# Two queues for the first transfers, and x ahead of the last memory blocks, in a two-layer hybrid attention kernel

## The chip, the cores and the metric

The kernel runs on one core of one Trainium2 chip. The metric is device time in microseconds of one execution; the runs of the kernel before took 297.54, 295.9 and 296.98 us, so the median is 296.98. Five engines work side by side, each in its own order: TensorE (PE; PEld are its weight loads), VectorE (DVE), ScalarE (ACT), GpSimd (POOL) and SyncE (SP), which here only issues transfers.

## The reference, cut to what matters

```python
def hybrid_layer(x, mem, norm_g, w_in, w_out, mem_norm_g, w_mem_kv, qk_g):
    h = rms_norm(x, norm_g)
    proj = jnp.einsum('btd,de->bte', h, w_in)
    ...
    a_q, a_k, a_v, a_g, b_q, b_k, b_v, b_g, m_q, m_g = jnp.split(proj, cuts, axis=-1)
    ...
    mkv = jnp.einsum('bmd,de->bme', rms_norm(mem, mem_norm_g), w_mem_kv)
    m_k, m_v = jnp.split(mkv, 2, axis=-1)
    qm = rms_norm(to_heads(m_q, N_HEADS_MEM), qk_g[4])
    km = rms_norm(to_heads(m_k, N_HEADS_MEM), qk_g[5])
    om = from_heads(memory_attention(qm, km, to_heads(m_v, N_HEADS_MEM)))

    y = jnp.concatenate([oa * jax.nn.silu(a_g), ob * jax.nn.silu(b_g), om * jax.nn.silu(m_g)], axis=-1)
    return x + jnp.einsum('bte,ed->btd', y, w_out)
```

Two such layers run one after the other. x and mem are 256 tokens of 1,024 columns in float32. Three kinds of attention (causal, dilated, and over the memory) share the projections of x; the memory's keys and values come from a projection of mem of their own.

## The kernel before, in words

Every product of activations and weights is made of three products of parts: an operand is split into a high part (`hi`, `xmh`; ScalarE casts it to a 12-bit form) and a low part (`lo`, `xml`; VectorE subtracts), and TensorE adds high x high, low x high and high x low (`products`, line 142). Weights arrive as raw tiles, one `raw` tile per unit, from a ring of three buffers (`RAW_BUFS`), are split (`split`, line 409; `hi` at line 422, `lo` at line 423), and used. A raw buffer is free again when the `lo` that reads it is done.

The projections stand in a fixed order: mkv (keys and values of the memory, 512 columns, two units of four row blocks), mq and mg (the memory attention's queries and gate, one unit of 1,024 KB each), then bq, bk, and so on (384 columns, two units each). The transfers stand in that order on SP, which issues them in order: one that waits for a free buffer holds those behind it.

The head of the first layer is the place of the change. The transposed memory (`memT`) comes in eight blocks of 128 rows, x in two halves of 128 tokens. All of it goes through SP: memory blocks and kv weights in turn, then x, then mq and mg, the untransposed memory, gains, bq. TensorE first runs 17 transposes of the identity (`warm`). The first four row blocks of mkv are then multiplied in float32 as they come (`whole`, line 477), the last four by parts: memory blocks 4 and 5, then 6 and 7 are split (`split_x`, line 174), and the weights with them. Then x's rows are scaled (`row_scale` and `normed_rows`: a square with a sum on ScalarE, `ms` on VectorE, a power on GpSimd, and `xn` on VectorE), transposed by TensorE in four groups of four (`transposed`), and split into `xmh` and `xml`. The scaled copy `xn` takes a buffer of the raw ring.

Behind this the memory attention starts: mq's two accumulators are squared, normalised and scaled (`normed`, line 253: `sq`, `hss`, `ms`, `hrs`, `t`, `qn`), then the keys (`kn`), and both are transposed (`pair_of_heads`, line 277) between the products of bq. Accumulators come from four PSUM banks (`acc`), so bq's take those of mq. Instructions passed through `pin` and `keep_in_program_order` stay in the order in which the code writes them; the other places are set by a scheduler when the program is built. TensorE's order is wholly that of the code.

Of the kernel before, what the change touches and what calls it, by code (L numbers as in the profile page):

```python
# [10 lines left out]
F32 = mybir.dt.float32  # L11
# [19 lines left out]
# microseconds of TensorE's own clock until a step of attention may follow  # L31
# [6 lines left out]
# Constants of the shapes alone: masks (an additive log of how many patterns hold a key) and rope tables.  # L38
# [26 lines left out]
def hybrid_kernel(ctx: ExitStack, tc: tile.TileContext, x, mem, mem_t, gains, w_in, w_out, w_mem_kv, qk_g, const, out):  # L65
# [11 lines left out]
    # ---- constants made on chip  # L77
# [4 lines left out]
    nc.scalar.activation(cp.tile([P, 16], F32, name="table"), mhalf, AF.Square)  # L82
    pinning = [True]

    def pin(ins):
        """Holds an instruction in its place in the order of its engine, where that is asked for."""
        return tc.keep_in_program_order(ins) if pinning[0] else ins
# [11 lines left out]
    def pe(ins, us):  # L99
        """TensorE follows the trace; its clock tells when what waits for other engines may come next."""  # L100
        tc.keep_in_program_order(ins)
        clock[0] += us
# [11 lines left out]
    def keep_warm(n):  # L114
        """TensorE's clock rises while it is busy."""
        for _ in range(n):
            pe(nc.tensor.transpose(warm[:, 0:P], ident, ident), 0)
# [3 lines left out]
    def poll():  # L121
        """The steps of attention whose operands should be there by now."""
# [19 lines left out]
    def products(groups, first, last, x_moves=False):  # L142
        """acc += x w by block of rows, x and w in two parts each: all products but that of the low parts."""
# [10 lines left out]
    def row_scale(src, t, name, junk):  # L154
        """rsqrt of the mean square of each token's row."""
# [9 lines left out]
    def transposed(src, k2, spare=False):  # L165
        """Two column blocks of both token tiles, by [column, token]."""
# [7 lines left out]
    def split_x(dst, v, g, k2):  # L174
        """Two column blocks, by [column, token], times the gains, in two parts of 12 bits each."""
# [9 lines left out]
    # ---- constants  # L185
# [7 lines left out]
    def prepare_tables(l):  # L193
        """A layer's gains times cosines and sines, the scale of the scores with those of the queries."""
# [17 lines left out]
    def project(xs, chunk, n):  # L212
        """Both token tiles times a chunk of columns."""
# [17 lines left out]
    def project_t(xs, chunk, n):  # L231
        """A chunk of columns of both token tiles, by [column, token]."""
# [20 lines left out]
    def normed(acc, n, dst, tables):  # L253
        """dst = the rms-normed (and rotated) heads of acc."""
# [22 lines left out]
    def pair_of_heads(qn, kn, pair, masks, v, gate, ready, finished):  # L277
        """Queries and keys by [dim, token]; then both heads, whose values share the columns of TensorE."""
# [43 lines left out]
    def head(me, s, spans, masks, pTs):  # L322
        """Softmax of a head, by [key, query] in the end."""
# [33 lines left out]
    # ---- the projections, in the order in which their weights come  # L357
# [12 lines left out]
    units = []  # (chunk, first row block, row blocks, columns)  # L370
# [8 lines left out]
    splits = []  # (unit, first row block, row blocks, columns)  # L379
# [5 lines left out]
    def loads():  # L385
        while loaded[0] < len(units):
# [12 lines left out]
            for b in range(0, nk, step):  # L399
                e = b + step  # L400
                pin(nc.sync.dma_start(raws[u][:, b:e],
                                      src[(a + b) * P:(a + e) * P, :].rearrange("(k p) n -> p k n", p=P)))
# [8 lines left out]
    def split(upto):  # L411
        """Weights in two parts of 12 bits each."""
# [15 lines left out]
    def weights():  # L428
        """The parts of the next chunk, one after another; those behind are under way."""
# [8 lines left out]
    # ---- the first arrivals, in the order of their use  # L438
    for k in range(KD):
        if k < 2 or k % 2 == 0:  # L440
            load_mem(k, k + 1 if k < 2 else k + 2)
        if k == 0:
            pin(nc.sync.dma_start(gT, gains))
        if k < 4 or k % 2 == 0:
            next(loading)
    for t in range(NT):
        pin(nc.sync.dma_start(x_sb[:, t], x[t * P:(t + 1) * P]))
    load(RAW_BUFS + 1)
# [7 lines left out]
    def next_mem(dst, g):  # L456
        """The next layer's memory, bit by bit."""
# [6 lines left out]
    for l in range(DEPTH):  # L464
        gx = gT[:, 8 * l:8 * l + 8]
        xn = wp.tile([P, NT, D], F32, tag="raw", name="xn", bufs=RAW_BUFS)
# [175 lines left out]
```

## Time and profile before

| | us |
|---|---|
| median of three runs | 296.98 |
| profiled execution, first to last instruction (span) | 296.5 |
| TensorE busy | 288.6 (97% of the span) |
| VectorE busy | 203.5 (69%) |
| ScalarE busy | 198.3 (67%) |
| GpSimd busy | 55.7 (19%) |

The profiled execution gives its span alone, 296.5 us; the timed runs lie between 295.9 and 297.54. A wait of an engine is named by who ended it. Matmul ends are modelled and a matmul overlaps the next one's start, so the starts of weight loads are the better clock for TensorE. The granted clock is shown as 1.00 in all stretches quoted.

### The profile page before, as it was taken

The numbers are of one execution on the slowest core, as the hardware profiler recorded it, in microseconds if no ns is written. First come the engines' busy times: TensorE is split into PE (matmuls) and PEld (weight loads), VectorE is DVE, ScalarE is ACT, GpSimd is POOL, SyncE is SP. The second block draws the span as 40 slices with busy tenths as digits, with TensorE's granted clock in tenths as the row PEclk, the third lists the DMA queues.
The fourth block names the chain that finished last, engine by engine and source line by source line (L and its number), as shares of the span: only waits on it lengthen the run. The fifth ranks groups of instructions, "written<-read, shape, count | busy, mean of one in ns | idle before, by whom it ended". The sixth has DMA issues, their size and how long they took to land.

```text
span 296.5 us, 4973 instructions
## 1 busy us (share of the span) xinstructions
PE 288.6 (97%) x1809; PEld 250.6 (85%) x1809; DVE 203.5 (69%) x454; ACT 198.3 (67%) x442; POOL 55.7 (19%) x73
## 2 busy tenths in 40 slices
PE   8989989999999999999999999999999999999994
PEld 6469989698988999977788999989898899987773
DVE  1468899977656997654475759879665699666413
ACT  2578888796878656988364654878587864698600
POOL 0013489130000330000001048703000023000000
PEclk9999999999999999999999999999999999999999
DMA  5999568235438067254307635650823715821003
GB/s 166 375 372 346 186 199 249 70 109 166 155 106 249 19 196 273 97 198 167 118 0 249 211 110 135 223 153 26 262 64 110 239 41 173 300 75 53 3 0 142
DMA packets 32777, 47.33 MB, mean 160 GB/s; under 512 B 1264, under 2 KB 27632, under 8 KB 32752
## 3 DMA queue, kind: packets, MB, share of 16 engines
q1 hardware_dynamic: 32752, 47.01, 48.6%
q8 instruction: 14, 0.23, 0.3%
q14 instruction: 11, 0.09, 0.1%
HBM read 45.96 MB, written 1.05 MB: 159 GB/s over the span
## 4 chain that ended last, share of the span: by engine, by line
PE 81%; DMA 7%; DVE 6%; ACT 2%; POOL 1%; issue 1%; SPq 1%; DVEq 0%; ACTq 0%
PE acc L107 65%; PE wk L110 8%; PE o L107 5%; PE wk L107 5%; DMA x_sb<-in_x_dram 3%; DMA raw<-in_w_in_dram 3%; DVE lo L423 2%; DMA raw<-in_w_mem_kv_dram 2%; POOL hrs L152 1%; DVE hss L259 1%; ACT hi L422 1%; DVE xn L454 0%; DVE ms L151 0%; ACT xn L157 0%; POOL r L152 0%
## 5 line engine op out<-in xcount | busy, mean ns | idle before, releaser
L423 DVE TENSOR_TENSOR lo<-raw,hi 128x768 fp32r<-128x768 f32 (+1 forms) x90 | 96.1, 1089 | 33.6 <-ACT hi L422 33.6
L422 ACT CAST hi<-raw 128x768 fp32r<-128x768 f32 (+1 forms) x90 | 82.9, 936 | 38.2 <-PE acc L107 25.8
L107 PE MATMUL acc<-hi,xmh 128*128 128x384 f32 (+2 forms) x248 | 66.1, 348 | 0.0
L107 PE MATMUL acc<-hi,xml 128*128 128x384 f32 (+2 forms) x248 | 62.7, 335 | 0.8 <-DVE xml L182 0.8
L107 PE MATMUL acc<-lo,xmh 128*128 128x384 f32 (+2 forms) x248 | 62.6, 334 | 0.0
L152 POOL TENSOR_TENSOR hrs<-ms,mhalf 128x6 f32<-128x6 f32 (+1 forms) x24 | 30.3, 1262 | 119.6 <-DVE ms L151 119.1
L107 PEld LDWEIGHTS acc<-hi,xmh 128*128 128x128 f32 x248 | 41.9, 189 | 5.3 <-issue 3.0
L107 PEld LDWEIGHTS acc<-hi,xml 128*128 128x128 f32 x248 | 44.1, 188 | 2.2 <-DVE xml L182 1.2
L107 PEld LDWEIGHTS acc<-lo,xmh 128*128 128x128 f32 x248 | 44.2, 188 | 1.0
L107 PE MATMUL acc<-hi,yT 128*128 128x512 f32 x128 | 41.5, 406 | 0.0
L107 PE MATMUL acc<-xmh,hi 128*128 128x256 f32 x128 | 29.7, 293 | 0.0
L337 ACT ACTIVATE pr<-pr,nm 128x128 f32<-128x128 f32 (+1 forms) x48 | 21.4, 446 | 12.2 <-DVE nm L335 12.2
L107 PE MATMUL acc<-xml,hi 128*128 128x256 f32 x128 | 28.4, 283 | 0.0
L107 PE MATMUL acc<-xmh,lo 128*128 128x256 f32 x128 | 28.4, 283 | 0.0
L107 PEld LDWEIGHTS acc<-hi,yT 128*128 128x128 f32 x128 | 23.0, 188 | 5.2 <-issue 0.7
L343 ACT ACTIVATE pr<-pr,rinv 128x128 f32<-128x128 f32 (+1 forms) x64 | 25.6, 461 | 0.0
L107 PE MATMUL acc<-lo,yT 128*128 128x512 f32 x64 | 25.3, 395 | 0.0
L107 PEld LDWEIGHTS acc<-xmh,hi 128*128 128x128 f32 x128 | 20.9, 191 | 0.7 <-issue 0.7
L107 PEld LDWEIGHTS acc<-xml,hi 128*128 128x128 f32 x128 | 21.1, 191 | 0.0
L107 PEld LDWEIGHTS acc<-xmh,lo 128*128 128x128 f32 x128 | 21.1, 191 | 0.0
L354 ACT COPY pT<-wk 128x384 f32<-128x384 f32 (+1 forms) x32 | 15.4, 503 | 6.5 <-PE wk L110 6.5
L335 DVE CUSTOM_DVE_ANT_0 pr<-wk,cst 128x128 f32<-128x128 f32 (+1 forms) x48 | 14.3, 353 | 5.3 <-PE wk L107 5.3
(75 smaller groups left out, 361.9 us busy)
## 6 DMA issues: line engine op xcount, KB each, us to landing
raw<-in_w_in_dram SPq DMA_DIRECT2D x24, 768.0 KB, 4.9
raw<-in_w_in_dram SPq DMA_DIRECT2D x8, 1024.0 KB, 5.5
raw<-in_w_out_dram SPq DMA_DIRECT2D x6, 1024.0 KB, 6.1
raw<-in_w_in_dram SPq DMA_DIRECT2D x4, 512.0 KB, 3.6
raw<-in_w_out_dram SPq DMA_DIRECT2D x4, 512.0 KB, 4.4
raw<-in_w_mem_kv_dram SPq DMA_DIRECT2D x2, 1024.0 KB, 5.0
raw<-in_w_mem_kv_dram SPq DMA_DIRECT2D x4, 256.0 KB, 4.9
raw<-in_w_mem_kv_dram SPq DMA_DIRECT2D x2, 512.0 KB, 7.2
```

The source lines that it names most:

```text
L107: pe(nc.tensor.matmul(out, a, b, start=start, stop=stop), us)
L110: pe(nc.tensor.transpose(out, a, ident), 0.109)
L152: pin(nc.gpsimd.tensor_tensor(dst, ms, mhalf[:, :n], op=ALU.pow))
L259: pin(nc.vector.tensor_reduce(ss, heads(sq), axis=AX.X, op=ALU.add))
L335: nc.vector.tensor_tensor_reduce(out=pr[:, spans[t]], in0=s[:, spans[t]], in1=masks[t], scale=-1.0, scalar=3e38, op0=ALU.add, op1=ALU.min, ...
L337: nc.scalar.activation(pr[:, spans[t]], pr[:, spans[t]], AF.Exp, scale=-1.0, bias=nm[:, t:t + 1], accum_out=sums[:, t:t + 1])
L343: nc.scalar.activation(pr[:, spans[t]], pr[:, spans[t]], AF.Copy, scale=rinv[:, t:t + 1])
L354: nc.scalar.copy(pT[:, :n], ps[:, :n])
L422: pin(nc.scalar.copy(hi, raw))
L423: pin(nc.vector.tensor_tensor(lo, raw, hi.bitcast(F32), op=ALU.subtract))
```

## The change

The six transfers of mkv's weights of the first layer are issued by ScalarE instead of SP, ahead of everything else there; the small activation that loads ScalarE's table moves behind them. On SP the halves of x stand ahead of memory blocks 4 and 5, and 6 and 7. The scaled copy of x in the first layer lies in a tile of the tag `yT1` rather than in the raw ring. The square, the scale and `xn` of each half of x are written between the splits of the last memory blocks, and TensorE transposes x ahead of the products of memory blocks 6 and 7. Splits of mq's weights follow the first two groups of x's parts. The rest of the diff takes out comments.

```diff
@@ -74,16 +74,15 @@
     mhalf = cp.tile([P, 16], F32, name="mhalf")
     nc.vector.memset(mhalf, -0.5)
-    nc.scalar.activation(cp.tile([P, 16], F32, name="table"), mhalf, AF.Square)
     pinning = [True]
...
@@ -398,8 +397,9 @@
             step = 1 if u == 0 else 2 if u == 1 else nk
             for b in range(0, nk, step):
                 e = b + step
-                pin(nc.sync.dma_start(raws[u][:, b:e],
-                                      src[(a + b) * P:(a + e) * P, :].rearrange("(k p) n -> p k n", p=P)))
+                queue = nc.scalar if u < 2 else nc.sync
+                pin(queue.dma_start(raws[u][:, b:e],
+                                    src[(a + b) * P:(a + e) * P, :].rearrange("(k p) n -> p k n", p=P)))
                 yield
 
     loading = loads()
...
@@ -435,16 +435,18 @@
             split(s + ahead[0])
             yield splits[s][1], splits[s][2], parts[s]
 
-    # ---- the first arrivals, in the order of their use
-    for k in range(KD):
-        if k < 2 or k % 2 == 0:
-            load_mem(k, k + 1 if k < 2 else k + 2)
-        if k == 0:
-            pin(nc.sync.dma_start(gT, gains))
-        if k < 4 or k % 2 == 0:
-            next(loading)
+
+    load(2)
+    next(loading)
+    nc.scalar.activation(cp.tile([P, 16], F32, name="table"), mhalf, AF.Square)
+    load_mem(0, 1)
+    pin(nc.sync.dma_start(gT, gains))
+    load_mem(1, 2)
+    load_mem(2, 4)
     for t in range(NT):
         pin(nc.sync.dma_start(x_sb[:, t], x[t * P:(t + 1) * P]))
+        load_mem(4 + 2 * t, 6 + 2 * t)
+    first_xn = sp.tile([P, NT, D], F32, tag="yT1", name="xn", bufs=1)
     load(RAW_BUFS + 1)
     pin(nc.sync.dma_start(mem_sb, mem.rearrange("(t p) c -> p t c", p=P)))
     load_gains(4, 6)
...
@@ -463,31 +465,33 @@
 
     for l in range(DEPTH):
         gx = gT[:, 8 * l:8 * l + 8]
-        xn = wp.tile([P, NT, D], F32, tag="raw", name="xn", bufs=RAW_BUFS)
+        xn = wp.tile([P, NT, D], F32, tag="raw", name="xn", bufs=RAW_BUFS) if l else first_xn
         xs = xm_tiles()
         if l == 0:
-            # the order of the arrivals, which holds every engine to it
+
             mem_xs = xm_tiles()
             whole.append(cp.tile([P, 4, T], F32, name="whole"))
             mkv, steps = project(mem_xs, weights(), 512)
             r_mem = []
             g = gT[:, 16:24]
             for k in range(4):
-                # float32 as it comes, while the parts of what follows are made
+
                 pin(nc.vector.tensor_scalar(whole[0][:, k], memT[:, k], g[:, k:k + 1], None, op0=ALU.mult))
                 next(steps)
-            for k2 in (4, 6):
+            for t, k2 in enumerate((4, 6)):
+                r = row_scale(x_sb, t, "r", xn[:, t])
                 split_x(mem_xs, memT[:, k2:k2 + 2], g, k2)
-                split(k2 // 2 + 1)
-            for t in range(NT):
-                normed_rows(t, xn)
-            split(SPLIT_BUFS)
-            for _ in range(2):
-                next(steps)
-            for k2 in range(0, KD, 2):
-                if k2 == 2:
-                    split(SPLIT_BUFS + 1)
-                split_x(xs, transposed(xn, k2, k2 == 6), gx, k2)
+                if t == 0:
+                    split(3)
+                pin(nc.vector.tensor_scalar(xn[:, t], x_sb[:, t], r, None, op0=ALU.mult))
+            split(4)
+            next(steps)
+            turned = [transposed(xn, k2, k2 == 6) for k2 in range(0, KD, 2)]
+            next(steps)
+            for k2, v in zip(range(0, KD, 2), turned):
+                split_x(xs, v, gx, k2)
+                if k2 < 4:
+                    split(SPLIT_BUFS + k2 // 2)
             mem_gain = gB[:, :, 4]
             pin(nc.gpsimd.tensor_scalar(mem_gain, mem_gain, 0.125, None, op0=ALU.mult))
             ahead[0] = SPLIT_BUFS - 1
```

What the scheduler makes of it follows at three places. The first is the head of SP's queue, where `memT` are the memory blocks and `raw<-in_w_mem_kv_dram` the kv weights; before:

```order
L95 DMA memT<-in_mem_t_dram 128x256
L443 DMA gT<-in_gains_dram 128x32
L401 DMA raw<-in_w_mem_kv_dram 128x512
L95 DMA memT<-in_mem_t_dram 128x256
L401 DMA raw<-in_w_mem_kv_dram 128x512
L95 DMA memT<-in_mem_t_dram 128x2x256
L401 DMA raw<-in_w_mem_kv_dram 128x512 x2
L95 DMA memT<-in_mem_t_dram 128x2x256
L401 DMA raw<-in_w_mem_kv_dram 128x2x512
L95 DMA memT<-in_mem_t_dram 128x2x256
L401 DMA raw<-in_w_mem_kv_dram 128x2x512
L447 DMA x_sb<-in_x_dram 128x1024 x2
L401 DMA raw<-in_w_in_dram 128x8x256 x2
```

And with the change, SP, and ScalarE's head beside it:

```order
L94 DMA memT<-in_mem_t_dram 128x256
L443 DMA gT<-in_gains_dram 128x32
L94 DMA memT<-in_mem_t_dram 128x256
L94 DMA memT<-in_mem_t_dram 128x2x256
L447 DMA x_sb<-in_x_dram 128x1024
L94 DMA memT<-in_mem_t_dram 128x2x256
L447 DMA x_sb<-in_x_dram 128x1024
L94 DMA memT<-in_mem_t_dram 128x2x256
L401 DMA raw<-in_w_in_dram 128x8x256 x2
```

```order
L401 DMA raw<-in_w_mem_kv_dram 128x512 x4
L401 DMA raw<-in_w_mem_kv_dram 128x2x512 x2
L441 ACT_TABLE_LOAD
L441 ACTIVATE table<-mhalf 128x16
L156 ACTIVATE xn,ss<-x_sb 128x1024
L178 ACTIVATE xmh<-memT,gT 128x256 x2
L422 CAST hi<-raw 128x1024
```

All kv weights went from SP to ScalarE, and x's halves stand third and second from the end of the first group on SP, each ahead of two memory blocks.

The second place is VectorE's head, from the float32 blocks (`whole`) to the first parts of x (`xml<-wk`); `lo<-raw,hi` are low parts of weights, `xn` is x scaled. Before, and with the change:

```order
L477 TENSOR_SCALAR whole<-memT,gT 128x256 x4
L182 SCALAR_TENSOR_TENSOR xml<-memT,gT,xmh 128x256 x2
L423 TENSOR_TENSOR lo<-raw,hi 128x1024
L182 SCALAR_TENSOR_TENSOR xml<-memT,gT,xmh 128x256 x2
L423 TENSOR_TENSOR lo<-raw,hi 128x1024
L151 TENSOR_SCALAR ms<-ss 128x1
L454 TENSOR_SCALAR xn<-x_sb,r 128x1024
L151 TENSOR_SCALAR ms<-ss 128x1
L454 TENSOR_SCALAR xn<-x_sb,r 128x1024
L423 TENSOR_TENSOR lo<-raw,hi 128x1024
L182 SCALAR_TENSOR_TENSOR xml<-wk,gT,xmh 128x256 x2
```

```order
L479 TENSOR_SCALAR whole<-memT,gT 128x256 x4
L150 TENSOR_SCALAR ms<-ss 128x1
L181 SCALAR_TENSOR_TENSOR xml<-memT,gT,xmh 128x256 x2
L423 TENSOR_TENSOR lo<-raw,hi 128x1024
L486 TENSOR_SCALAR xn<-x_sb,r 128x1024
L150 TENSOR_SCALAR ms<-ss 128x1
L181 SCALAR_TENSOR_TENSOR xml<-memT,gT,xmh 128x256 x2
L486 TENSOR_SCALAR xn<-x_sb,r 128x1024
L423 TENSOR_TENSOR lo<-raw,hi 128x1024
L181 SCALAR_TENSOR_TENSOR xml<-wk,gT,xmh 128x256 x2
L423 TENSOR_TENSOR lo<-raw,hi 128x1024
```

The second `lo`, that of mkv's last two row blocks, stood ahead of both `xn` and stands behind both, and the square's follow-up `ms` of each half moved up between the splits of the memory blocks.

The third place is VectorE from the low parts of mg (`128x1024 x2`) to the normalisation of the memory's queries (`hss`, `t`, `qn`); `lo<-raw,hi 128x768` are low parts of bq. Before, and with the change:

```order
L423 TENSOR_TENSOR lo<-raw,hi 128x1024 x2
L151 TENSOR_SCALAR ms<-ss 128x1
L423 TENSOR_TENSOR lo<-raw,hi 128x768
L259 TENSOR_REDUCE hss<-sq 128x4
L151 TENSOR_SCALAR ms<-hss 128x4
L263 TENSOR_TENSOR t_336<-acc,gB 128x256
L273 TENSOR_TENSOR qn<-t_336,hrs 128x256
L259 TENSOR_REDUCE hss<-sq 128x4
L151 TENSOR_SCALAR ms<-hss 128x4
L263 TENSOR_TENSOR t_347<-acc,gB 128x256
L423 TENSOR_TENSOR lo<-raw,hi 128x768
```

```order
L423 TENSOR_TENSOR lo<-raw,hi 128x1024 x2
L150 TENSOR_SCALAR ms<-ss 128x1
L423 TENSOR_TENSOR lo<-raw,hi 128x768 x2
L258 TENSOR_REDUCE hss<-sq 128x4
L150 TENSOR_SCALAR ms<-hss 128x4
L262 TENSOR_TENSOR t_336<-acc,gB 128x256
L272 TENSOR_TENSOR qn<-t_336,hrs 128x256
L258 TENSOR_REDUCE hss<-sq 128x4
L150 TENSOR_SCALAR ms<-hss 128x4
L262 TENSOR_TENSOR t_347<-acc,gB 128x256
L423 TENSOR_TENSOR lo<-raw,hi 128x768
```

Both low parts of bq's first half stand ahead of the first `hss` now, where one did; further on, the one that stood ahead of the second `kn` is gone from there.

## Rows read from the trace of the kernel before

**Rows 1.** The page, its first part (busy time of each engine and its share of the span) and, of its sixth part, the row of the 1,024 KB transfers of input weights over the whole run (count, KB each, median us from issue to landing).

```profile
PE 288.6 (97%) x1809; PEld 250.6 (85%) x1809; DVE 203.5 (69%) x454; ACT 198.3 (67%) x442; POOL 55.7 (19%) x73
raw<-in_w_in_dram SPq DMA_DIRECT2D x8, 1024.0 KB, 5.5
```

**Rows 2.** The view of waits, of TensorE's matmuls in the first 62 us: line and tile that waited, engine and tile waited for: us in total, times, longest.

```profile
PE warm L117 <- POOL ident masks.py:199: 1.3, 1, 1.3
PE wk L110 <- DVE kn L273: 0.9, 1, 0.9
PE acc L107 <- DVE xml L182: 0.8, 2, 0.6
PE wk L110 <- DVE xn L454: 0.6, 1, 0.6
PE wk L107 <- ACT pT L354: 0.4, 1, 0.4
```

**Rows 3.** The chain of work that ended last, in order of time: start us, us, what.

```profile
21.25 7.86 DMA raw<-in_w_in_dram
29.18 0.84 ACT hi L422
30.05 0.96 DVE lo L423
...
40.13 0.47 DVE kn L273
40.65 0.33 PE wk L110
```

**Rows 4.** The timeline of the first 25 us, TensorE's weight loads (each stands just ahead of its matmul): start us, us, engine, line, operation, count, and in brackets the idle time before it and what ended it. `warm` are the transposes that only keep TensorE busy, `acc<-raw,whole` the first four memory blocks, `acc<-hi,xmh` x4 the next ones, `wk<-ident,xn` the transposes of x, the last row the first products of the second projection.

```profile
1.34 3.49 PEld L117 LDWEIGHTS warm<-ident 128*128 128x128 f32 x17 [1.34 <-POOL ident masks.py:199]
...
11.88 0.19 PEld L107 LDWEIGHTS acc<-raw,whole 128*128 128x128 f32 x1 [0.24 <-issue]
12.86 0.76 PEld L107 LDWEIGHTS acc<-hi,xmh 128*128 128x128 f32 x4 [0.79 <-ACT hi L422]
...
18.23 0.14 PEld L110 LDWEIGHTS wk<-ident,xn 128*128 128x128 f32 x1
20.95 0.30 PEld L107 LDWEIGHTS acc<-hi,xmh 128*128 128x128 f32 x2
```

**Rows 5.** The view of windows: stretch, its length, then busy us (and count) of PE, PEld, DVE, ACT and POOL, the granted clock, the DMA engines' busy share, and GB/s.

```profile
1.50:2.50 1.00, 1.00 (x6) 1.00 (x7) 0.00 (x0) 0.72 (x2) 0.00 (x0) 1.00 0.59 144
2.50:3.50 1.00, 1.00 (x6) 1.00 (x5) 0.35 (x1) 0.00 (x0) 0.00 (x0) 1.00 0.33 110
...
4.50:5.50 1.00, 1.00 (x5) 0.86 (x4) 0.35 (x1) 0.00 (x0) 0.00 (x0) 1.00 0.73 167
5.50:6.50 1.00, 1.00 (x2) 0.33 (x1) 0.00 (x0) 0.00 (x0) 0.00 (x0) 1.00 0.84 180
...
10.00:12.50 2.50, 2.50 (x7) 0.95 (x5) 0.88 (x2) 1.64 (x3) 0.00 (x0) 1.00 1.02 377
```

**Rows 6.** DMA issues, each asked for the stretch of its own issue: the memory blocks 6 and 7 (issued at 5.50 us), the second half of x (7.87), mq (8.78), mg (16.11) and the first half of bq (21.25). Columns: tile, queue, count, KB each, us from issue to landing.

```profile
memT<-in_mem_t_dram SPq DMA_DIRECT2D x1, 256.0 KB, 6.9
x_sb<-in_x_dram SPq DMA_DIRECT2D x1, 512.0 KB, 8.4
raw<-in_w_in_dram SPq DMA_DIRECT2D x1, 1024.0 KB, 10.5
raw<-in_w_in_dram SPq DMA_DIRECT2D x1, 1024.0 KB, 6.1
raw<-in_w_in_dram SPq DMA_DIRECT2D x1, 768.0 KB, 7.9
```

**Rows 7.** The timeline from 10 to 20 us, ScalarE and VectorE: high and low parts of two memory blocks, the low part of the last kv weights, the scaling of x.

```profile
10.49 0.91 ACT L179 ACTIVATE xmh<-memT,gT 128x256 fp32r<-128x256 f32 x2 [8.26 <-DMA memT<-in_mem_t_dram]
11.03 0.88 DVE L182 SCALAR_TENSOR_TENSOR xml<-memT,gT,xmh 128x256 fp32r<-128x256 f32 x2 [2.65 <-ACT xmh L179]
...
14.86 1.23 DVE L423 TENSOR_TENSOR lo<-raw,hi 128x1024 fp32r<-128x1024 f32 x1
...
18.55 0.75 DVE L454 TENSOR_SCALAR xn<-x_sb,r 128x1024 f32<-128x1024 f32 x1 [0.68 <-POOL r L152]
```

**Rows 8.** The timeline of SP's issues: the first kv weights, and mg.

```profile
1.63 0.42 SPq L401 DMA_DIRECT2D raw<-in_w_mem_kv_dram  x1
...
16.11 0.38 SPq L401 DMA_DIRECT2D raw<-in_w_in_dram  x1
```

**Rows 9.** The timeline from 33 to 41 us on VectorE, GpSimd and TensorE: the normalisation of the memory's queries (`t<-acc,gB`) and of its keys (`ms`, `hrs`), the low part of a weight, and TensorE's first products of bq and the last transpose ahead of the wait for kn.

```profile
33.54 0.42 DVE L263 TENSOR_TENSOR t<-acc,gB 128x256 f32<-128x256 f32 x1
...
38.75 0.17 DVE L151 TENSOR_SCALAR ms<-hss 128x4 f32<-128x4 f32 x1
39.15 0.95 DVE L423 TENSOR_TENSOR lo<-raw,hi 128x768 fp32r<-128x768 f32 x1
...
38.99 1.11 POOL L152 TENSOR_TENSOR hrs<-ms,mhalf 128x4 f32<-128x4 f32 x1 [1.28 <-DVE ms L151]
33.90 0.62 PE L107 MATMUL acc<-hi,xmh 128*128 128x384 f32 x2
39.45 0.27 PE L110 MATMUL wk<-ident,qn 128*128 128x128 f32 x1
```

## The prediction

> **What bounds the kernel now.** I read the page first: TensorE is busy 97% of the span [rows 1], so a change to the start can only pay by removing idle time of TensorE or add some. The view of waits shows where that is: after the first wait for the identity there are only five, 2.7 us in all, for kn (0.9), xml (0.8), xn (0.6) and pT (0.4), all before 56 us [rows 2]. From there to the end TensorE runs without a wait, so whatever the first 56 us gain or lose arrives unchanged at the end. The chain shows which of the five is real: it leaves TensorE at 21.25, runs through the transfer of bq's first half, its cast at 29.18, its low part on VectorE at 30.05 and down VectorE's queue to kn, whose transpose TensorE runs at 40.65 [rows 3]. TensorE had been ready at 39.45 + 0.1 [rows 9]. A gain earlier than that only lengthens this wait, unless the chain moves too. The weight loads show the head: fp32 products start when the warming transposes end (4.81) and run without a gap to 12.86 [rows 4], so an earlier first transfer gives TensorE nothing there.
>
> **The change, part by part.**
>
> *Transposes of x ahead of the last memory products.* Sixteen transposes move ahead of twelve products; the count is the same. Before, TensorE waits for xn at 18.5 and then for xml, whose operands had just been transposed. Now the twelve products (12.86 to 18.23 is 24 of them, so 2.7 us) [rows 4] lie between transposes and use, which hides xml: -0.8. Before the transposes it waits for xn still. All of this lies ahead of kn, so it is worth nothing unless kn comes earlier.
>
> *Two queues.* Six issues move from SP to ScalarE, ahead of its table load; ScalarE first works at 10.49 [rows 7], so they are covered. The 4.2 MB of kv weights, memory and x are the same transfers. Their last landing before is x's second half, 7.87 + 8.4 = 16.27 [rows 6]; now it is memory blocks 6 and 7, behind both halves of x (before: 5.50 + 6.9 = 12.4). When they land is what I can't read and must bound. From 2.5 to 3.5 us the engines moved 110 GB/s and from 4.5 to 6.5 167 and 180, against 377 from 10 to 12.5 [rows 5]. At 377 the first stretch loses 0.7 us, the second 1.1. The first is a single queue starting up (share 0.33) and should go with a second queue. In the second the engines were 0.73 and 0.84 busy at half the rate, so packets were slow, and I give back half: 16.27 - 0.7 - 0.55 = 15.0. Bounds: nothing gained, 16.3; all at 377 from the first bytes, which fall in the stretch from 1.5 to 2.5, so 1.7 + 11.1 = 12.8.
>
> The Trainium skill (DMA: Bandwidth & Descriptors, "Issuing engines are not separate DMA queues") says that transfers issued by several engines run on the same 16 DMA engines, and that a second issuer saves only issuing time. No row of this trace has a second issuer. Here that time is 0.9 us, since kv's first weights go out as SP's first instruction rather than at 1.63 [rows 8]; by the rule alone the blocks land at 15.4 and the sum below is 0.4 us worse.
>
> *VectorE's order.* The low part of the last kv weights ends before at 14.86 + 1.23 = 16.1, ahead of both scalings of x. Now it stands behind xml of blocks 6 and 7 and the second xn. xmh to xml of two blocks takes 10.49 to 11.91, 1.4 us; xn 0.75, lo 1.23 [rows 7]. So it ends at 15.0 + 1.4 + 0.75 + 1.23 = 18.4.
>
> *What waits for that.* mg's transfer takes the raw buffer of the last kv weights: before it is issued at 16.11, directly behind that lo [rows 8], while mq (8.78 + 10.5 = 19.3) still fills the queue [rows 6]. Queued behind it on SP are mem, gains and bq's first half. Freeing x's scaled copy from the raw buffers lets bq go without waiting for the transposes (21.25 before), but it still stands behind mg, and before it was not late: its transfer needed 7.9 us because others were ahead. Now mg goes out at 18.4. mq, at most 2.9 us behind the blocks (the distance of mq and mg before, 19.3 to 22.2), lands at 17.9, and the queue is dry. The nearest row for an issue into a dry queue is the median of the 1,024 KB transfers, 5.5 us [rows 1]; bounds are 2.9 (the queue never dry) and 6.1 [rows 6]. So mg lands at 23.9 instead of 22.2, and bq's first half 6.95 later as before (22.2 to 29.15): 30.85. That is +1.7.
>
> *The second place on VectorE.* Both low parts of bq's first half now stand ahead of the normalisation of the memory's queries; before, only one did. The other three stay in front of kn. The one removed at 39.15 lay beside GpSimd's 38.99 to 40.10, for which kn waited anyway [rows 9], so it cost nothing; ahead of the normalisation it costs its 0.85 to 0.95. Landing to kn's transpose was 40.65 - 29.15 = 11.5; now 12.35, so 43.2: +2.55. TensorE's first wait on this chain comes sooner: bq's products need the PSUM bank that `t<-acc,gB` reads, before 33.54 to 33.96 against TensorE's 33.90 [rows 9], just in time. With the chain 2.55 later TensorE stops there, and for kn again.
>
> *The pT wait* (0.4) hung on ScalarE and VectorE work that now gets time while TensorE stands: gone. Sum: 2.55 - 0.4 = +2.15 us. The profiled execution's span is 296.5; the median of the timed runs is 296.98, 0.5 above, which I take for what lies around the span. Forecast 296.98 + 2.15 = 299.1. Below I use the sum as 2.15 + (landing of blocks 6 and 7 - 15.0).
>
> **Rivals.**
>
> *No change.* The two queues cure the whole slow start: landing at 12.8, sum -0.05, 296.9. For it: the shares under 1 before 6.5 us. Against it: rates were low even where the engines were busy. Break-even is a landing at 12.85; at 14.35 it is 1.5 us slower.
>
> *Faster.* The chain to kn drops off the path. If transfers also run closer together from mg to bq, and bq lands by 25.7, kn is ready at 38.1, when TensorE, without the 0.6 and 0.8, arrives there (39.55 - 1.4). All five waits but the first go: -2.7, 294.3. For it: bq no longer waits for x's copy. Against it: bq would have to land 3.4 us earlier, while mg is issued later in every case worked out above.
>
> *Slower still.* x between the memory blocks starves the head: the two queues share the engines without gain, blocks 4 to 7 come at 16.3, and TensorE stands at the fifth block as well. Sum 2.15 + 1.3 = 3.45, 300.4. It decides if the stretch to 10 us shows no more GB/s than before.
>
> **How the numbers follow.** Measurement can tell 0.5%, 1.5 us, from no change. Forecast 0.40, no change 0.34, faster 0.14, slower still 0.12. Of the forecast's case, whose own range (landing 14.0 to 15.9) is 298.1 to 300.0, a small part, 0.04, falls under 1.5 us; and part of the faster case gains less than 1.5 us. So faster 0.13, same 0.39, slower 0.48. The range reaches from the middle between the no-change and faster cases (296.9 and 294.3), 295.7, to the bound of the slower one, 300.5; about 0.1 lies below and 0.08 above.
>
> **What would show it.** Right: blocks 6 and 7 land near 15.0, mg is issued near 18.4 directly behind lo, bq's first half lands near 30.9; TensorE's waits have a new one at bq's first products (VectorE's t, 1 to 3 us), kn's transpose is near 43.2, and the xml waits are gone. Wrong: mg issued before 17, bq landed by 29, or TensorE at kn without a wait; or a landing of x's second half after 16 us, which gives the last rival. Also wrong if a wait behind 60 us appears or goes, since I carry everything to the end unchanged.

## The result and the profile after

The changed kernel took 299.94 us (median of four runs, 299.59 to 300.6), the kernel before beside it 297.06 (295.9 to 297.54): a ratio of 1.0104, interval 1.008 to 1.0127, some 2.9 us slower. The forecast was 299.1, with a range of 295.7 to 300.5. The profiled execution has a span of 297.8 us and took 299.59.

Waits of TensorE in the first 70 us (line and tile that waited, engine and tile waited for: total, times, longest); they answer to [rows 2]:

```profile
PE acc L106 <- DVE t L262: 2.3, 2, 1.7
PE warm L116 <- POOL ident masks.py:199: 1.3, 1, 1.3
PE acc L106 <- ACT hi L422: 1.0, 1, 1.0
PE wk L109 <- DVE xn L486: 0.5, 1, 0.5
```

kn, xml and pT are gone; in their place TensorE stands 2.3 us at bq's first products for `t`, the reader of the PSUM bank that they take. Why `t` is late stands in the chain of work that ended last (start, us, what), which answers to [rows 3]:

```profile
6.80 7.79 DMA memT<-in_mem_t_dram
...
16.28 0.04 DVE xn L486
16.31 0.63 issue
16.95 1.23 DVE lo L423
18.18 0.02 issue
18.19 0.37 SPq L401
...
18.61 0.58 SPq L451
...
19.80 10.22 DMA raw<-in_w_in_dram
...
30.11 0.84 ACT hi L422
...
31.85 0.95 DVE lo L423
...
34.47 0.42 DVE qn L272
...
35.33 0.43 DVE t L262
35.76 0.14 issue
35.90 6.87 PE acc L106 x29
42.77 0.44 PE wk L109 x4
...
59.95 4.37 PE acc L106 x24
```

Read downwards, each transfer's landing being its start and its length together: memory blocks 6 and 7 land at 14.59; the second `xn`, then the low part of the last kv weights; that ends at 18.18 and SP issues mg at 18.19 (16.11 before [rows 8]); mem and gains follow, then bq's first half at 19.80, which lands at 30.02 (29.11 before [rows 3]); its high and low parts, `qn`, `t`, and TensorE at 35.90. From 58 us on next to nothing differs. The same 24 products, in the chain of before:

```profile
58.49 4.37 PE acc L107 x24
```

They stand 238.01 us from the end of that trace and 237.85 from the end of the one after. So the two traces are 1.46 us apart at these products, and no wait behind 60 us has appeared or gone.

The DMA engines after, by windows (columns as in [rows 5]):

```profile
2.50:3.50 1.00, 1.00 (x6) 1.00 (x5) 0.00 (x0) 0.00 (x0) 0.00 (x0) 1.00 1.09 380
...
5.50:6.50 1.00, 1.00 (x3) 0.38 (x2) 0.35 (x1) 0.01 (x1) 0.00 (x0) 1.00 1.10 389
...
15.00:20.00 5.00, 4.55 (x29) 3.78 (x28) 4.50 (x9) 3.80 (x8) 0.74 (x1) 1.00 0.42 127
17.00:18.00 1.00, 0.92 (x8) 0.92 (x9) 1.00 (x2) 0.33 (x1) 0.00 (x0) 1.00 0.00 0
20.00:25.00 5.00, 5.00 (x37) 4.72 (x36) 4.86 (x9) 4.34 (x8) 0.00 (x0) 1.00 1.07 395
```

The two queues do cure the slow start (380 and 389 GB/s, before 110 and 180 [rows 5]). What they gain goes in the hole from 15 to 20 us: mq has landed at 17.3, mg waits for a buffer until 18.19, and from 17 to 19 us nothing moves at all.

### The profile page after: what moved, and what is told of

Same layout as the page of the kernel before. It is cut to its first block, busy times and chain, and to the rows that moved or that the text cites. A ratio compares the mean times of both kernels' runs of the same rounds, so it can differ in the third digit from the quotient of the medians.

```text
span 297.8 us, 4971 instructions
## 1 busy us (share of the span) xinstructions
PE 289.0 (97%) x1809; PEld 251.9 (85%) x1809; DVE 203.6 (68%) x454; ACT 198.9 (67%) x442; POOL 54.4 (18%) x73
## 4 chain that ended last, share of the span: by engine, by line
PE 87%; DMA 8%; DVE 2%; SPq 1%; issue 1%; POOL 1%; ACT 0%; DVEq 0%; ACTq 0%
PE acc L106 70%; PE wk L109 7%; PE wk L106 5%; PE o L106 5%; DMA memT<-in_mem_t_dram 4%; DMA raw<-in_w_in_dram 3%; DVE lo L423 1%; POOL hrs L151 0%; ACT hi L422 0%; SPq L94 0%; DVE xn L486 0%; POOL r L151 0%; DVE hss L258 0%; SPq L451 0%; SPq L189 0%
## 5 line engine op out<-in xcount | busy, mean ns | idle before, releaser
L422 ACT CAST hi<-raw 128x768 fp32r<-128x768 f32 (+1 forms) x90 | 82.9, 937 | 36.5 <-PE acc L106 26.6
L106 PE MATMUL acc<-hi,xmh 128*128 128x384 f32 (+2 forms) x248 | 67.0, 352 | 3.3 <-DVE t L262 2.3
L106 PEld LDWEIGHTS acc<-hi,xmh 128*128 128x128 f32 x248 | 42.5, 191 | 9.0 <-ACT hi L422 3.7
L106 PEld LDWEIGHTS acc<-hi,xml 128*128 128x128 f32 x248 | 44.8, 190 | 1.0
L336 ACT ACTIVATE pr<-pr,nm 128x128 f32<-128x128 f32 (+1 forms) x48 | 21.4, 448 | 12.4 <-DVE nm L334 12.2
L342 ACT ACTIVATE pr<-pr,rinv 128x128 f32<-128x128 f32 (+1 forms) x64 | 25.7, 463 | 0.0
```

Source lines behind the costliest of these rows:

```text
L106: pe(nc.tensor.matmul(out, a, b, start=start, stop=stop), us)
L336: nc.scalar.activation(pr[:, spans[t]], pr[:, spans[t]], AF.Exp, scale=-1.0, bias=nm[:, t:t + 1], accum_out=sums[:, t:t + 1])
L342: nc.scalar.activation(pr[:, spans[t]], pr[:, spans[t]], AF.Copy, scale=rinv[:, t:t + 1])
L422: pin(nc.scalar.copy(hi, raw))
```

## The experiments

Theory A is the forecast's: the loss is that chain, from the late low part through mg's late transfer to `t` and kn. Rivals: B, part of it lies outside the span and comes with a second issuing engine (the time was 1.8 us above the span here, and the forecast had taken 0.5 for the kernel before); C, it is TensorE's clock, which fell to 0.50 at 37 us. Twelve kernels ran, one of them the kernel before again. They were timed on other occasions than the changed kernel, each beside the kernel before, whose median was then 297.17 to 297.47. Two sets of runs of that one kernel (e0) had medians 0.8 us apart, so a smaller difference of medians decides little by itself.

**e1, the queues alone**, on the kernel before (the activation that loads ScalarE's table moves behind these issues; marked `...`):

```diff
...
+queue = nc.scalar if u < 2 else nc.sync
-pin(nc.sync.dma_start(raws[u][:, b:e],
+pin(queue.dma_start(raws[u][:, b:e],
...
```

> The kernel before with one edit: the first projection's weights are issued by ScalarE, on a second queue, and ScalarE's table load stands behind those issues; order of work and of the other transfers unchanged. Theory A (the loss is the chain: low part of the last kv weights late on VectorE, mg's transfer late, bq's first half late, TensorE waits at bq's products): VectorE's order is the one of before, so that low part ends by 16.5 us, mg is issued by 16.5, bq's first half lands by 29.2, there is no wait for VectorE's t at bq's first products, and the span is 295.5 to 296.5. Theory B (about 1.3 of the 2.9 us lie outside the span and come with a second issuing engine): time less span is 1.8, so a time of 297.3 to 298.3 with such a span. Rival to B (time less span is the same for every kernel): the time is that of the kernel before or up to 1 us less.

298.87 us, ratio 1.0045 (1.0025 to 1.0066): on the old order the second queue costs some 1.5 us. B falls: time less span is 1.73 to 1.86 us in every run listed of every kernel, those of the kernel before included. A's numbers miss too: VectorE's order is the old one, yet mg goes out no earlier than 17.9, as the kv weights themselves are late. The last ones are cast at 15.59 (13.77 before), and TensorE waits 1.7 us for the high part of those ahead:

```profile
13.48 1.04 ACT L422 CAST hi<-raw 128x1024 fp32r<-128x1024 f32 x1 [4.10 <-DMA raw<-in_w_mem_kv_dram]
...
15.59 1.05 ACT L422 CAST hi<-raw 128x1024 fp32r<-128x1024 f32 x1 [0.25 <-DMA raw<-in_w_mem_kv_dram]
```

(timeline of e1, ScalarE: start, us, instruction, idle time before it and what ended it). That they are late because they share the DMA engines with memory and x is likely but not shown.

**e2, the order alone**: the changed kernel, with every transfer on SP. The kv weights' issues also go back between those of memory and x, one by one (marked `...`).

```diff
-queue = nc.scalar if u < 2 else nc.sync
+queue = nc.sync
...
```

> The changed kernel with its transfers all on SP's queue, memory, kv weights and x interleaved; the order of work is that of the changed kernel (second xn ahead of the low part of the last kv weights, transposes of x ahead of the last products). Theory A: the low part still ends at 18 us or later, mg is issued right behind it, TensorE waits for VectorE's t at bq's first products 3 to 6 us in all, and the span is 297.5 to 299. Theory B: with one issuing engine the time less span is 0.5, so a time of 298.0 to 299.5, under that of the changed kernel; rival to B: time less span is 1.8 here too, and the time is 299.3 to 300.8.

300.05 us, ratio 1.0077 (1.0051 to 1.0103), span 298.2; waits for `t` again 2.3 us; the low part ends at 18.5, bq's first half is cast at 30.53. With the changed order the loss is there whole on one queue, and the second queue adds and saves nothing that shows. The two parts do not add up: each alone makes the kernel slower (e1 by 1.5 us), and together they cost no more than the order.

**e3, a late transfer on ScalarE**, on the kernel before:

```diff
-pin(nc.sync.dma_start(cst, const))
+pin(nc.scalar.dma_start(cst, const))
```

> The kernel before with one transfer, the table of constants (cst), issued by ScalarE instead of SP, so that a second queue exists and nothing at the start depends on it. Theory B: the span stays within 0.7 us of 296.5 and the time rises by 1.0 to 1.6 us over the kernel before. Rival (a second issuing engine costs nothing outside the span): time and span within 0.7 us of the kernel before.

298.83 us, ratio 1.0047 (1.0027 to 1.0066). The rise looks like B, but the span rose with it (296.6 to 298.6 over the runs, time less span as ever). Not a clean isolation: when built, the scheduler also moved VectorE's and ScalarE's work ahead of kn, and TensorE's wait for kn is 1.8 us instead of 0.9.

**e4, TensorE kept busy** ahead of bq's first products, on the changed kernel:

```diff
+if l == 0 and kind == 2:
+    fill = o_p.tile([P, T], F32, tag="o", name="fill")
+    for _ in range(20):
+        pe(nc.tensor.transpose(fill[:, 0:P], ident, ident), 0)
```

> The changed kernel with 20 more transposes of the identity on TensorE, results unused, ahead of bq's first products of the first layer, where TensorE stands waiting. They keep TensorE busy between 33 and 36 us. Theory C (the fall of the granted clock to 0.50 from 37 to 40 us costs most of the loss): the clock stays at 1.00 there and the time falls by 1.4 to 1.8 us. Theory A (kn, ready at 42.4, sets the end of this stretch with or without the slow clock): the clock stays at 1.00, TensorE reaches kn's transposes 1.5 us sooner and waits there about 0.6 to 1.2 us for VectorE's kn, and the time falls by 0.3 to 0.7 us only.

300.14 us, ratio 1.0086 (1.0057 to 1.0114). Windows of the changed kernel, then of e4 (the figure ahead of the last two is the granted clock):

```profile
33.00:34.00 1.00, 0.39 (x3) 0.19 (x1) 0.64 (x3) 1.00 (x4) 0.58 (x1) 1.00 1.06 370
34.00:35.00 1.00, 0.23 (x1) 0.00 (x0) 0.53 (x2) 1.00 (x3) 0.43 (x1) 1.00 1.04 361
35.00:36.00 1.00, 0.10 (x1) 0.13 (x2) 0.97 (x4) 1.00 (x3) 0.50 (x1) 1.00 1.05 375
...
38.00:39.00 1.00, 1.00 (x5) 1.00 (x5) 0.90 (x4) 1.00 (x4) 0.61 (x1) 0.50 0.00 0
```

```profile
35.00:36.00 1.00, 0.89 (x8) 0.63 (x6) 0.96 (x4) 1.00 (x3) 0.10 (x1) 1.00 0.94 330
...
38.00:39.00 1.00, 1.00 (x8) 1.00 (x7) 1.00 (x3) 0.90 (x3) 0.29 (x2) 1.00 0.08 25
```

The clock stays up and nothing is gained: e4's waits have a new 0.9 us for kn. The traces say it more sharply than the medians can: from the start of bq's cast to the 24 products of 58 us it is 29.82 us in e4 (30.50 to 60.32) and 29.84 in the changed kernel (30.11 to 59.95). C falls. The low clock ran beside a wait that would have come anyway. A's small gain of 0.3 to 0.7 did not come either.

**e5, the low part ahead of the second xn**, on the changed kernel:

```diff
-if t == 0:
-    split(3)
+split(3 + t)
...
-split(4)
```

> The changed kernel with one place exchanged on VectorE: the low part of the last kv weights stands ahead of the second scaling of x, so it ends some 0.75 us sooner (17.4 instead of 18.2) and mg is issued at 17.4. Theory A (bq is late because mg's transfer is issued late, into a dry queue): bq's first half lands 0.5 to 0.75 us sooner (29.3 to 29.5), the waits for VectorE's t at bq's first products shrink by as much, and the time falls by 0.5 to 0.8 us against the changed kernel. Rival (the order on VectorE between 31 and 42 us sets kn and the landing matters little): within 0.3 us of the changed kernel.

300.53 us, ratio 1.0105 (1.0079 to 1.0132): no gain. It is no test of A, as the low part, waiting for its high part, ended at 17.84, 0.3 us sooner instead of 0.75; the later xn made TensorE wait 2.1 us for it, and bq's first half was cast at 30.69.

**e6, the second low part of bq's first half behind the queries' normalisation**, on the changed kernel:

```diff
+if l == 0:
+    split(10)
```

> The changed kernel with the second low part of bq's first half behind the normalisation of the memory's queries on VectorE; four low parts still stand ahead of kn, as in the changed kernel. The forecast's step on the second place says that this low part costs 0.85 us: then TensorE's waits for VectorE's t shrink from 2.3 to about 1.4 us, kn comes 0.5 to 0.85 us sooner, and the time falls by as much. Rival (its place does not matter to kn, as the same work stands ahead of it): the waits for t shrink, kn comes within 0.2 us of 42.4, and the time stays within 0.3 us of the changed kernel.

301.7 us, ratio 1.0143 (1.0117 to 1.017): 1.8 us slower than the changed kernel. TensorE still stands 1.7 us at the same bank; the view puts this down to ScalarE's `sq`, but `sq` had ended at 32.0, and `t` ended at 35.38, just ahead of TensorE's start at 35.53. Then TensorE waits 2.5 us for kn. VectorE's and GpSimd's timeline of e6 on the way to kn:

```profile
34.09 0.43 DVE L272 TENSOR_TENSOR qn<-t,hrs 128x256 f32<-128x256 f32 x1 [0.79 <-POOL hrs L151]
36.18 0.43 DVE L272 TENSOR_TENSOR qn<-t,hrs 128x256 f32<-128x256 f32 x1 [0.80 <-POOL hrs L151]
38.89 1.99 POOL L151 TENSOR_TENSOR hrs<-ms,mhalf 128x4 f32<-128x4 f32 x1 [0.72 <-DVE ms L150]
40.91 0.42 DVE L272 TENSOR_TENSOR kn<-t,hrs 128x256 f32<-128x256 f32 x1 [0.90 <-POOL hrs L151]
43.29 0.46 DVE L272 TENSOR_TENSOR kn<-t,hrs 128x256 f32<-128x256 f32 x1 [0.57 <-POOL hrs L151]
```

VectorE stands 3.1 us for GpSimd's `hrs` here, in the changed kernel 1.7 (0.80 + 0.38 + 0.50). The count of low parts ahead of kn is four in both. The second gap, 0.80, has lost the low part that stood in it. The third, 0.90, has another cause: a low part does lie there (39.05, 0.95 us), but GpSimd's `hrs` took 1.99 us instead of 1.12, and the trace does not show why.

kn ends 1.4 us later than in the changed kernel (43.75 against 42.39), 0.5 of it from a later cast of bq (30.61 against 30.11). More is lost behind it. Two lines of each chain, the changed kernel's and then e6's, and a window of e6 (the figure ahead of the last two is the granted clock):

```profile
43.20 1.06 PE acc L106 x6
44.70 2.10 PE acc L106 x12
```

```profile
44.14 1.65 PE acc L106 x6
46.64 2.65 PE acc L106 x12
```

```profile
45.00:46.00 1.00, 1.00 (x5) 0.90 (x4) 1.00 (x2) 1.00 (x3) 1.00 (x2) 0.50 0.00 0
```

TensorE was busy for 0.44, 0.00 and 0.19 us of the three microseconds from 41 to 44, and then its clock stood at 0.50. The work from kn's transpose to the next products `wk<-qkT` is the same in both and takes 5.4 us (43.81 to 49.23) instead of 3.8 (42.93 to 46.72). So most of what e6 loses between the traces (its 24 products come at 62.08 instead of 59.95) is the clock and a long `hrs`, and e6 is no clean test of where the low part should stand.

**e8, mem ahead of mg** on SP, on the changed kernel:

```diff
-load(RAW_BUFS + 1)
+load(RAW_BUFS)
 pin(nc.sync.dma_start(mem_sb, mem.rearrange("(t p) c -> p t c", p=P)))
 load_gains(4, 6)
+load(RAW_BUFS + 1)
```

> The changed kernel with the transfers of mem (1 MB) and of two rows of gains issued on SP ahead of mg's instead of behind it; they need no raw buffer, so they fill the queue while mg's waits for the low part of the last kv weights. Theory A: the engines move over 300 GB/s from 15 to 18.5 us, where the changed kernel's moved 127 GB/s from 15 to 20; bq's first half lands by 27.5 instead of 30.0; ScalarE casts it as soon as it is done with mg's, at 28.4; TensorE's waits for VectorE's t shrink to under 1 us, kn comes 1.3 to 1.8 us sooner, and the time falls by 1.3 to 1.8 us, to 298.1 to 298.7. Rival (the second place on VectorE alone holds kn up): the landing moves and the time falls by less than 0.5 us.

297.72 us, ratio 1.0012 (0.9995 to 1.0029): 2.2 us off the changed kernel, more than A asked for, and no measurable difference from the kernel before. Its windows and waits, from an execution of 298.5 us, 0.8 above its median:

```profile
15.00:20.00 5.00, 4.42 (x29) 3.66 (x27) 4.45 (x8) 3.56 (x8) 0.56 (x1) 1.00 0.99 350
```

```profile
PE wk L109 <- DVE kn L272: 0.9, 1, 0.9
...
PE acc L106 <- DVE t L262: 0.2, 1, 0.2
```

mg's own transfer is no earlier for it: SP issues it at 19.47, and it lands at 25.10. But mem's 1 MB has used the hole and no longer stands between mg and bq, so ScalarE can cast bq's first half at 29.03, straight behind mg's and without a wait for a transfer. Filling the hole alone pays, and what pays is bq's arrival, not mg's.

**e9, e5, e6 and e8 together.** 

> The three edits of e5, e6 and e8 together. Theory A: bq's first half lands by 26.5, both places on VectorE are undone, kn is ready by 40.3, no wait for t remains, and the time falls by 2.0 to 2.8 us against the changed kernel, to 297.2 to 298.0, within 0.6 us of the kernel before. If the head of the changed kernel (waits for hi and xn, 1.5 us in all) is no longer covered, that is what remains on top; if the time falls below 296.5, the waits that the kernel before had for xml and pT were worth something after all.

299.6 us, ratio 1.0075 (1.0046 to 1.0105). The landing is early (cast at 27.93) and no wait for `t` is left, but the two edits on VectorE give back 1.9 of e8's 2.2 us. Its `hrs` ahead of kn took 1.98 us too, at 36.27.

**e0, the kernel before once more.** 

> The kernel before, unchanged, profiled a second time. Its 45 other runs spread over 296.4 to 299.4 us with spans 1.8 us less, so the execution of rows 1 to 9 (span 296.5) was one of about 298.3, a slow one of them. Expected: a span of 294.8 to 297.6; if it is near the median's 295.6, bq's first half lands sooner than 29.15 us and the wait for kn is shorter than 0.9 us, which would say that the spread is that of the arrivals. If the landing and the kn wait are those of rows 3 and 9 with a span near 295.6, the spread sits behind 56 us.

297.95 us, ratio 1.0011 (0.9983 to 1.0038). Its profiled execution took 298.66 with a span of 296.9, again over a microsecond above the median of the kernel before. bq's first half landed at 28.67, 0.44 sooner than in rows 3, and the wait for kn was 0.3. Yet the 24 products came at 58.88, 0.4 later: a new wait of 0.4 for kv weights stands ahead, and one of 0.2 behind. The spans of this kernel go down to 294.4; no execution near that has a trace.

**e10, x's scaled copy apart** from the raw buffers, on the kernel before:

```diff
...
+first_xn = sp.tile([P, NT, D], F32, tag="yT1", name="xn", bufs=1)
...
-xn = wp.tile([P, NT, D], F32, tag="raw", name="xn", bufs=RAW_BUFS)
+xn = wp.tile([P, NT, D], F32, tag="raw", name="xn", bufs=RAW_BUFS) if l else first_xn
```

> The kernel before with one part of the change alone: x's scaled copy stands apart from the raw buffers, so bq's transfer need not wait for the transposes of x. All orders and the single queue are those of the kernel before. The forecast's step says that this is worth nothing, since bq stands behind mg and mem in a queue that is full: then bq's issue moves from 21.3 to about 17.7 us, its landing by less than 0.5 us, and the time stays within 0.5 us of the kernel before. Rival (the queue has gaps from 24 to 28 us, 318 and 296 GB/s, because bq's halves were issued late): landing 0.7 to 1.0 us sooner, the wait for kn falls to 0.2 or less, and the time falls by 0.6 to 0.9 us.

297.62 us, ratio 1.0008 (0.9987 to 1.0029). bq is issued at 16.98 and lands at 28.79, 0.3 sooner: worth nothing that shows, as the forecast said.

**e12, mg in a buffer of its own**, on the changed kernel:

```diff
+if u == 3:
+    raws[u] = sp.tile([P, nk, n], F32, tag="yT0", name="raw", bufs=1)
...
```

> The changed kernel with mg's weights landing in a buffer of their own, so that their transfer waits for nobody; all orders as in the changed kernel. Theory A (the whole loss is mg's transfer behind the low part of the last kv weights): mg is issued by 10 us, lands by 20, the queue has no gap from 15 to 20, bq's first half lands by 25 and is cast as soon as ScalarE comes to it, there is no wait for t and none or at most 0.4 us for kn, and the time falls by 2.7 to 3.3 us against the changed kernel, to 296.6 to 297.3, at or under the kernel before. Rival (something else in the changed kernel, such as the waits for hi and xn at its head, costs on its own): more than 298.0 although the landing comes early.

296.46 us, ratio 0.9976 (0.9958 to 0.9993): 3.5 us off the changed kernel, and under the kernel before. All of TensorE's waits in the first 70 us:

```profile
PE acc L106 <- ACT hi L425: 1.9, 1, 1.9
PE warm L116 <- POOL ident masks.py:199: 1.3, 1, 1.3
```

mg is issued at 9.24 and lands at 21.3, bq's first half lands at 26.6 and is cast at 27.76. The landings are later than A asked for (20 and 25), and the cast follows the landing by 1.2 us, but no wait for `t` or kn is left, and the 24 products come at 57.63, 2.3 us sooner than in the changed kernel and 0.9 sooner than in the trace of before. So the head's loss goes with the wait for the buffer, although the wait for hi grew from 1.0 to 1.9. That settles A's first link.

The rest of the gain lies elsewhere. From the 24 products to the end e12 takes 237.2 us, e13 below 237.1, every other trace 237.8 to 238.2. These two kernels lay mg's buffer in the tile of one part of `yT`, and their 192 products that read `yT` took 402 and 391 ns each (by high and by low part of the weights) instead of 404 and 394 in the changed kernel and 406 and 395 before: 66.0 us in all instead of 66.6 and 66.8. That the place of the tile does it is argued; no run separates it. Without it e12 would stand near the kernel before, not under it.

**e13, both buffers apart on the kernel before** (the edits of e10 and e12). 

> The kernel before with both buffers apart, x's scaled copy (as in e10) and mg's weights (as in e12); its single queue, its order of transfers and its order of work are kept. It differs from e12 by the change's queues and orders alone. Theory A with a full queue: in the kernel before mg never found a dry queue, so its own buffer buys nothing there; bq's first half lands near 28.8 as in e10 and the time is that of e10, 297.2 to 297.9. Then the 296.5 of e12 need the change's own part (both queues, x ahead) as well as the buffer. Rival: the buffer alone gives it, and the time is 296.2 to 296.8 here too.

296.28 us, ratio 0.9966 (0.9947 to 0.9984): the rival has the time right. It is that of e12, without the change's queues and order. bq's first half moved only to 28.20 (chain of e13):

```profile
16.76 11.44 DMA raw<-in_w_in_dram
...
28.28 0.84 ACT hi L425
```

But the gain over the kernel before, 1.1 us, is about what these two kernels save behind 58 us (0.9), and by an estimate a typical execution of the kernel before casts bq at 28.3 as well (its median 297.38, less 1.8 around the span, less 238.0 behind the 24 products, less the 29.3 between cast and products). So A's reason, that mg found no dry queue there and its own buffer buys little in the head, is not refuted.

12 runs of e13 lie between 295.94 and 296.81, where the kernel before beside them had 296.22 to 299.51. This may mean that the spread comes from mg's issue, but e2 and e6, whose mg still waits in the ring, spread over only 0.5 and 1.1 us in six runs each; no trace shows it.

**All traces together.** From the start of the cast of bq's first half to the 24 products at 58 us it takes, with the old order of work, 29.31 us before (29.18 to 58.49), 29.31 in e1 (29.61 to 58.92), 29.32 in e10 (28.87 to 58.19) and 29.31 in e13 (28.28 to 57.59). With the changed order it takes 29.84 in the changed kernel (30.11 to 59.95) and 29.81 to 29.87 in e2, e4, e5, e8 and e12, whose casts lie anywhere from 27.76 to 30.69. So the time of that cast sets all that follows, and the 1.46 us between the two traces come apart: 0.93 from bq's later cast, 0.53 from the order of work behind it. e0, e3, e6 and e9 take longer, by delays of their own (30.1 to 31.5).

## Why the prediction was right, step by step

*Two queues.* Blocks 6 and 7 were put at 15.0 and landed at 14.59. The Trainium skill (DMA: Bandwidth & Descriptors, "Issuing engines are not separate DMA queues") holds that a second issuer saves issuing time alone. By the forecast's estimate of that time, 0.9 us, they would then have landed at 15.4. For the whole time that is borne out here with the changed order: 300.05 with one queue, 299.94 with two. The rate at the start differs, 176 GB/s from 2.5 to 3.5 us with e2's one queue and 380 with two, but by 2.5 us two engines had also issued about twice the bytes of one, so this may itself be issuing time saved; no run separates the two. (A slip in the working: kv's first weights go out as ScalarE's first instruction, not SP's.)

*VectorE's order and mg.* The low part was to end at 18.4 and ended at 18.18; mg was issued at 18.19 into a dry queue, and ScalarE, waiting for it, began its cast at 23.25, 5.1 us later (forecast 5.5). bq's first half landed at 30.02 instead of 30.85: these two terms were 0.8 us too long in all.

*The second place on VectorE.* From bq's landing to the end of kn 12.4 us (42.39 - 30.02) against 11.5 before (40.60 - 29.11): 0.9, the forecast said 0.85. The size was right, the reason half. The low part that lay at 39.15 covered a wait for GpSimd, as the forecast says; without it VectorE stands 0.50 us there, and its waits for `hrs` on the way to kn are 1.7 us instead of 1.2 (0.79 + 0.39). So it costs where it went because it no longer fills a gap. The traces support this; e6, which put the low part elsewhere, is no clean test of it.

*TensorE's waits.* A wait for `t` of 1 to 3 us: 2.3. "For kn again": no. From bq's first products to the transposes TensorE took 6.9 us (35.90 to 42.77), before 5.3 (33.90 to 39.23), part of it at the halved clock, and came when kn had just been made (42.39). "TensorE at kn without a wait" was named as a sign of being wrong, and it occurred; but TensorE came only 0.2 us behind kn, and e4, with the clock up, has the wait again, 0.9 us. So the path is the one forecast. kn's transpose came at 42.77, or 42.93 for the last row of the four as in [rows 3], +2.28 against the forecast's +2.55.

*The pT wait.* It went. At 58 us the two traces are 1.46 us apart, so 0.8 was won between kn and there, twice the 0.4 of the view of waits. It was won at the same stop: the eight products `wk<-qkT` around the wait for pT took 2.24 us before (53.99 to 56.23) and 1.50 after.

*Around the span.* This term was wrong. "0.5 above, which I take for what lies around the span": it is 1.8, so the execution of [rows 1 to 9] took some 298.3 us, 1.3 above the median. Between the two traces the sum came to 1.3 (spans) to 1.5 (at 58 us), not 2.15; between the medians it is 2.9. So the forecast came near partly by two errors that offset each other: terms some 0.7 too long, worked out from an execution 1.3 slower than the typical one. That part is luck. The mechanism is the one forecast, and e8 and e12 show it. What a typical execution of the kernel before does otherwise than rows 1 to 9 stays open.

*The rivals.* The case of no change needed a landing at 12.85; it was 14.59. Faster needed bq by 25.7. For slower still the stretch to 10 us was to show no more GB/s than before; it showed more. No wait behind 60 us came or went.

## What to carry to other kernels

When transfers share a ring of buffers, look up for each one which instruction frees its buffer: here 2 us of delay in one subtraction emptied the queue and brought bq's weights 0.9 us later. Fill such a hole with a transfer that needs no buffer (2.2 us here), or give the waiting one a buffer of its own (2.3 us in the head of e12; another 0.7 came from behind it). Ask what a profiled execution itself took before a median is compared with its span. And compare traces at marks along the way, here the cast of bq and the products at 58 us: they tell which stage a gain came from, where the totals cannot.

## What was not expected of the hardware

TensorE's granted clock fell to 0.50, the lower of its two levels (1.2 of 2.4 GHz), from 37 to 40 us, after three microseconds in which it was busy for 0.39, 0.23 and 0.10 us; in e12 it fell too, behind the 1.9 us wait for hi:

```profile
15.00:16.00 1.00, 1.00 (x4) 0.81 (x4) 1.00 (x4) 0.89 (x4) 0.00 (x0) 0.63 1.10 349
16.00:17.00 1.00, 1.00 (x4) 0.72 (x3) 0.94 (x3) 1.00 (x2) 0.80 (x1) 0.50 1.10 346
17.00:18.00 1.00, 1.00 (x4) 0.81 (x3) 1.00 (x2) 0.23 (x1) 0.00 (x0) 0.50 1.11 350
```

(windows of e12, the clock ahead of the last two columns). In e4 the wait was filled, the clock held, and nothing was gained: e4 shows that the first fall cost nothing. A like fall in e6 cost 1.6 us, since no other wait lay beside it. For that of e12 it is only argued that it was free: kn ended at 40.10 and was transposed at 40.16, so a TensorE that came sooner would have waited there.
